# A modulation section summed in the sparse loop, a shorter burst table and an earlier branch in a one-core RG-LRU + SSD + PEER layer

## The chip, the cores and the metric

The kernel runs on one core of a Trainium2 chip. The metric is the device time of one execution in microseconds, as the median of several runs of the same program. A lower time is better. Everything is computed in float32; the large products are made from float32 weights that are split on the chip into a high and a low part.

## The reference

One layer with two sub-layers, both under adaLN modulation: a vector `c` gives six sections of 2,048 numbers each (shift, scale and gate of both sub-layers) by `silu(c) @ w_ada + b_ada`. There are 256 tokens of width 2,048.

```python
mod = silu(c) @ w_ada + b_ada                 # 6 sections of 2048
h   = rms_norm(x, norm1_g) * (1 + scale1) + shift1
proj = h @ w_in                               # RG-LRU and SSD heads
mix = concat([lru_out, ssd_out]) @ w_out      # 4096 -> 2048
x   = x + gate1 * mix
h2  = rms_norm(x, norm2_g) * (1 + scale2) + shift2
# PEER: 8 heads, product keys, 16 experts a head out of 128 * 128
act = gelu(einsum("td,thkd->thk", h2, u_tab[expert]))
out = einsum("thk,thkd->td", gate * act, v_tab[expert])
x   = x + gate2 * out                         # gate2: the last section
return rms_norm(x, final_norm_g)
```

So a token has 128 experts, and an expert is one row of `u_tab` and one of `v_tab` (2,048 floats, 8,192 bytes each). Section 5 of the kernel's `mod`, gate2, is needed only when the output of PEER is added to `x`.

## The kernel before

**Stages, in the order of the program.** First the modulation sections 0 and 1 are made on TensorE (PE). Then comes the input projection with the RG-LRU and SSD heads (to 549 us in the profile), the output projection (549 to 772 us, 64 slots: 32 that make the first 1,024 columns of the output, lines L885 to L887, and 32 for the others, L931 and L932), the queries, and PEER, which takes the rest.

**The weight pipeline.** Every 512 KB piece of a large weight is loaded by SyncE (SP) into one of four buffers `raw`, copied to a rounded high part by ScalarE (ACT, L149) and subtracted to a low part by VectorE (DVE, L158) into one of four buffers `hl`; PE then uses both parts. The subtraction of a piece frees its `raw` and so issues the load of a later piece. A stage can run ahead by what these buffers hold.

**Modulation sections 2 to 5** are sums on DVE: one step (`ada_step`, L391 and L394) loads 128 rows of 1,024 columns of `w_ada`, 512 KB, into one of two buffers `adr`, and adds them, times `c`, to the accumulator `adacc`; after 16 steps a closing of small matmuls on PE (`fin`, L403), due two slots later, sums over the 128 partitions. How often a step is taken is set by three rates: ADA_SSD and ADA_LRU steps a slot in the input projection, ADA_OUT in the output projection. The list `adq` has 7 × 16 = 112 steps: sections 2 to 4 and the first half of section 5. The second half of section 5 is summed later by `gate2_tick` (loads L1341 of 256 KB, DVE L1353 and L1355 on 128 x 512, closing L1366), in steps 32 to 63, one in each of the ticks 0 to 33 of PEER's sparse u loop but two.

**PEER in two parts.** An expert's key is its number modulo 128. Keys 0 to 99 are sparse, keys 100 to 127 dense.

- *Sparse u loop*: 25 calls of `u_quad`, each of 8 ticks, 200 ticks in all; a tick takes one 512 KB weight and makes 12 matmuls of 128 x 512 (L1496 to L1498). It makes the scores of all tokens for four keys, which are stored to DRAM: table `ad0` for keys 0 to 47, `ad1` for 48 to 99. Meanwhile DVE, ACT and PE build lists (`l_step`, `g_step`, the first around L1410 to L1425): for every block of 128 tokens (2) and group of 32 tokens (4) the entries are packed in chunks of 128, GA = 14 chunks for keys 0 to 47, and GB = 15 for keys 48 to 99. Entries that don't fit set `flag`, and a guarded branch (`spill`) adds them one token at a time.
- *Bursts*: one list chunk of all four groups is a quad, NQD = 2 × 29 = 58 of them, in the order block 0's first 14, block 1's 29, block 0's other 15. GpSimd (POOL) gathers for a quad four row buffers of 128 rows of `v_tab` (`v_feed`, L1544, up to 1 MB each, an empty slot moves nothing) and four columns of scores (`w_feed`, L1557); ACT and DVE make the burst's weights Wz from them (`w_make`: L1579, L1580, L1570, L1571), and PE does the 16 matmuls of the burst (`v_quad`, L1591; the records show 32). The function `tick` places a burst: the pacing formula with `sq["all"]`, the made weights, and two ticks after the rows were issued. Everything on POOL goes in program order, so a gather that waits for its buffer or for a stored table holds up what stands behind it. The row buffers are tk (4 of them), vq4 and vx; vq5 and vq6 are cleared (L1533) and added after the u loop.
- *Dense u*: 28 slots of two ticks each (`u_slot`, L454 and L456). *Dense v*: two halves of 28 slots (`v_slot`, L1693). Bursts go on through both; `merge` (L1720, L1722, L1725) adds a finished 128 x 512 sum to the rows in `R["t"]`; between the two halves stands the branch (L1809), after it the final RMSNorm, `final`.

The order of instructions on each engine is fixed when the program is built: what `tick`, `defer` and `mid` emit where is decided by counts, not by time. `gate2_tick`, `open_sparse` (it starts the bursts, when the lists are ready and `ad0` is stored) and `tick` are called in every tick of `u_quad`.

## Time and profile before

| what | value |
|---|---|
| runs | 2103.86, 2112.83, 2099.82 us; median 2103.86 |
| profiled execution | 2116.66 us, of which the span of the engines' work is 2114.7 |
| granted TensorE clock, mean | 0.969 |
| instructions in the span | 33,428 |
| HBM read, written | 650.45 MB, 17.34 MB |

The profiled execution is a single run, 12.8 us above the median of the others. Its own time is the span and some 2 us around it. The views that matter here are the engines' busy times; windows, which give for a stretch of time its length, each engine's busy time with the number of instructions in brackets, the granted clock of TensorE, the busy share of the DMA engines and the rate; the waits of PE by what ended them (microseconds in total, times, longest); the timeline, with the start and the length of an instruction and in square brackets the idle time before it and what ended that; and the chain of waits that ended last. PEld is the loading of weights into the array, which runs beside PE.

### The profile page before, as it was taken

The numbers are of one execution on the slowest core, as the hardware profiler recorded it, in microseconds if no ns is written. First come the engines' busy times: TensorE is split into PE (matmuls) and PEld (weight loads), VectorE is DVE, ScalarE is ACT, GpSimd is POOL, SyncE is SP. The second block draws the span as 40 slices with busy tenths as digits, with TensorE's granted clock in tenths as the row PEclk, the third lists the DMA queues.
The fourth block names the chain that finished last, engine by engine and source line by source line (L and its number), as shares of the span: only waits on it lengthen the run. The fifth ranks groups of instructions, "written<-read, shape, count | busy, mean of one in ns | idle before, by whom it ended". The sixth has DMA issues, their size and how long they took to land. (4 is left out here: it accounts for less than half of the span.)

```text
span 2114.7 us, 33428 instructions
## 1 busy us (share of the span) xinstructions
PE 1987.9 (94%) x12488; PEld 1558.1 (74%) x12488; DVE 1399.9 (66%) x2184; ACT 898.0 (42%) x1366; POOL 745.6 (35%) x629
## 2 busy tenths in 40 slices
PE   7999999999999999999999899899998799999796
PEld 4789989989998889888787466566665476666563
DVE  3378888898978778999898666565433244455444
ACT  3346666677633345444443233243232233333333
POOL 0013344322202110000011666556644566656452
PEclk9999999999999999999999899999999899999998
DMA  9967767777889965796567799999997899989993
GB/s 388 406 230 249 229 214 242 242 254 275 284 317 325 322 210 193 247 301 223 185 200 265 245 386 394 360 339 403 392 389 271 290 418 419 396 314 411 357 422 143
DMA packets 255050, 642.19 MB, mean 304 GB/s; under 512 B 28096, under 2 KB 132720, under 8 KB 227696
## 3 DMA queue, kind: packets, MB, share of 16 engines
q1 hardware_dynamic: 203408, 390.38, 53.6%
q0 software_dynamic: 40832, 215.51, 25.3%
q10 hardware_dynamic: 10640, 34.08, 4.4%
q8 instruction: 100, 1.64, 0.3%
q14 instruction: 70, 0.57, 0.1%
HBM read 650.45 MB, written 17.34 MB: 316 GB/s over the span
## 5 line engine op out<-in xcount | busy, mean ns | idle before, releaser
L149 ACT ACTIVATE hl<-raw 128x1024 fp32r<-128x1024 f32 x554 | 585.0, 1059 | 1027.2 <-PE b L1498 250.6
L158 DVE TENSOR_TENSOR hl<-raw,hl 128x1024 fp32r<-128x1024 f32 x554 | 697.8, 1263 | 354.1 <-ACT hl L149 266.9
L454 PE MATMUL b<-H,hl 128*128 128x512 f32 x1056 | 379.9, 403 | 12.4 <-DVE lsm L1570 11.4
L1496 PE MATMUL b<-hl,H 128*128 128x512 f32 x800 | 325.0, 406 | 4.5 <-ACT X L1502 4.3
L1557 POOL DMA_INDIRECT lsm<-ad,X x232 | 275.8, 1189 | 116.3 <-issue 75.3
L1498 PE MATMUL b<-hl,H 128*128 128x512 f32 x800 | 315.2, 394 | 0.0
L1497 PE MATMUL b<-hl,H 128*128 128x512 f32 x800 | 315.2, 394 | 0.0
L456 PE MATMUL b<-H,hl 128*128 128x256 f32 x1056 | 296.7, 281 | 2.4 <-DVE hl L158 2.4
L454 PEld LDWEIGHTS b<-H,hl 128*128 128x128 f32 x1056 | 199.3, 189 | 73.4 <-issue 24.5
L1591 PE MATMUL b<-tk,Wz 128*32 128x512 f32 x1072 | 226.1, 618 | 17.8 <-DMA tk<-in_v_t,X 8.1
L1544 POOL DMA_INDIRECT tk<-in_v_t,X x134 | 151.9, 1133 | 231.3 <-PE b L1591 138.7
L456 PEld LDWEIGHTS b<-H,hl 128*128 128x128 f32 x1056 | 200.3, 190 | 4.0 <-DVE hl L158 3.1
L1496 PEld LDWEIGHTS b<-hl,H 128*128 128x128 f32 x800 | 152.5, 191 | 56.5 <-issue 22.0
L1591 PE MATMUL b<-vq,Wz 128*32 128x512 f32 x520 | 186.7, 616 | 7.8 <-DMA vq<-in_v_t,X 7.8
L1498 PEld LDWEIGHTS b<-hl,H 128*128 128x128 f32 x800 | 152.3, 190 | 33.7
L1693 PE MATMUL b<-hl,X 128*128 128x512 f32 x672 | 160.9, 398 | 15.4 <-DVEq L1809 10.9
L1497 PEld LDWEIGHTS b<-hl,H 128*128 128x128 f32 x800 | 153.0, 191 | 29.4
L1693 PEld LDWEIGHTS b<-hl,X 128*128 128x128 f32 x672 | 126.5, 191 | 55.9 <-issue 24.1
L394 DVE SCALAR_TENSOR_TENSOR adacc<-adr,cact,adacc 128x1024 f32<-128x1024 f32 x105 | 142.3, 1356 | 36.2 <-DMA adr<-in_w_ada 35.8
L809 PE MATMUL b<-H,hl 128*128 128x256 f32 x560 | 161.6, 289 | 0.4 <-DVE ggt L466 0.4
L811 PE MATMUL b<-H,hl 128*128 128x256 f32 x560 | 158.4, 283 | 1.3 <-DVE hl L158 1.3
L810 PE MATMUL b<-H,hl 128*128 128x256 f32 x560 | 158.3, 283 | 0.0
(385 smaller groups left out, 3225.3 us busy)
## 6 DMA issues: line engine op xcount, KB each, us to landing
raw<-in_u_t SPq DMA_DIRECT2D x228, 512.0 KB
raw<-in_w_in SPq DMA_DIRECT2D x146, 512.0 KB
adr<-in_w_ada SPq DMA_DIRECT2D x112, 512.0 KB
adw<-in_w_ada SPq DMA_DIRECT2D x64, 512.0 KB
raw<-in_w_o SPq DMA_DIRECT2D x64, 512.0 KB
raw<-in_w_q SPq DMA_DIRECT2D x32, 512.0 KB
raw<-in_u_t ACTq DMA_DIRECT2D x28, 512.0 KB
raw<-in_v_t SPq DMA_DIRECT2D x28, 512.0 KB
```

The costliest lines, as they stand in the source:

```text
L149: act.activation(t[:, 0], r, AF.Copy)
L158: dve.tensor_sub(t[:, 1], r, t[:, 0].bitcast(FT))
L454: pe.matmul(ps, w[:, 0, c], x[:, k].rearrange("p a b -> p (a b)"), start=(k == first), stop=False, skip_group_check=True)
L456: pe.matmul(ps[:, :256], w[:, 1, c], x[:, k, 0], start=False, stop=(k == 15), skip_group_check=True)
L809: pe.matmul(ps, wh, hT[:, k, 0, :], start=(k == 0), stop=False)
L811: pe.matmul(ps, wl, hT[:, k, 0, :], start=False, stop=(k == 15))
L1496: pe.matmul(o, hh, w[:, 0, :, kk], start=(k == 0), stop=False)
L1497: pe.matmul(o, hl_, w[:, 0, :, kk], start=False, stop=False)
L1498: pe.matmul(o, hh, w[:, 1, :, kk], start=False, stop=(k == 15))
L1557: pool.indirect_dma_start(wA[:, n % 32:n % 32 + 1], None, adf[i], bass.IndirectOffsetOnAxis(ap=LW[:, tb, g, m:m + 1], axis=0), bounds_chec ...
L1591: pe.matmul(sb[c][32 * g:32 * g + 32, :], Wz[:, q % NW, g], buf[4 * q + g][:, c * 512:(c + 1) * 512], start=(m == a), stop=(m == b - 1), s ...
L1693: pe.matmul(ob[tb * 2 + c], w[:, i, s], v[:, k, c * 512:(c + 1) * 512], start=(jj == 0 and (i, k) == (0, 0)), stop=(jj == JD - 1 and k == 1))
```

## The change

Five things are edited.

1. The whole of section 5 goes to `gate2_tick`: `adq` ends with section 4 (96 steps), ADA_OUT is 0.74, and `gt` starts at step 0 in place of 32. A gate step is taken in each tick before 40 and in every second one after it, so its 64 steps last from tick 0 to tick 86. `open_sparse` waits for all 64 and for their closings to be issued.
2. GB is 14: 28 chunks in each block and 56 quads.
3. The two row buffers vq5 and vq6 are cleared and added inside the u loop, in the first tick in which the bursts are on and no list work is pending. The words "behind the gates" in the change's name mean the buffers' place in memory (`ohr`, `X01`), which the lists and gate sums used before.
4. `w_make` may begin the weights of quad `sq["n"] + 1`, one earlier; a burst has to be two ticks behind its made weights (`mt`) as well as its rows. `lsm` is 112 wide in place of 96.
5. The branch with `spill` stands between the dense u and the dense v loop, behind a `wsplit()` for slot 0. `spill` loads its own rows of x and gate2, and stores x back, before the rows for the merges are loaded.

```diff
-GA, GB = 14, 15
+GA, GB = 14, 14
...
-ADA_SSD, ADA_LRU, ADA_OUT = 0.65, 1.1, 1.0
+ADA_SSD, ADA_LRU, ADA_OUT = 0.65, 1.1, 0.74
...
-    adq = [(s, h, k) for s, h in ((2, 0), (2, 1), (3, 0), (3, 1), (4, 0), (4, 1), (5, 0)) for k in range(16)]
+    adq = [(s, h, k) for s in (2, 3, 4) for h in range(2) for k in range(16)]
...
-    lsm = pr.tile([128, 96], FT, name="lsm")
+    lsm = pr.tile([128, 112], FT, name="lsm")
...
-    gt = {"n": 32, "ld": 32, "fin": 2}
+    gt = {"n": 0, "ld": 0, "fin": 0}
...
-            gate2_tick()
-            if sq["ready"] and not sq["on"] and sq["stored"][0]:
+            if it < 40 or it % 2 == 0:
+                gate2_tick()
+            if sq["ready"] and not sq["on"] and sq["stored"][0] and gt["n"] == 64 and not pedue:
                 open_sparse()
+            if sq["on"] and not sq["rows7"] and not (bg or bg2 or any(stages)):
+                sq["rows7"] = True
+                add_row(s1.tile([128, D], FT, name="vq5", tag="ohr"))
+                add_row(keep.tile([128, D], FT, name="vq6", tag="X01"))
             tick()
...
             sq["made"] += 1
+            mt[q] = sq["it"]
...
-        if q >= NQD or q > sq["n"] or sq["w"] < 4 * q + 4 or sq["it"] < wt[q] + 6:
+        if q >= NQD or q > sq["n"] + 1 or sq["w"] < 4 * q + 4 or sq["it"] < wt[q] + 6:
...
-                and sq["g"] >= 4 * q + 4 and sq["it"] >= rt[q] + 2 and not (q == GA + GL - 1 and sq.get("rows", n) > n - 8)):
+                and sq["g"] >= 4 * q + 4 and sq["it"] >= max(rt[q], mt[q]) + 2 and not (q == GA + GL - 1 and sq.get("rows", n) > n - 8)):
...
             sp.dma_start(g2d.rearrange("o (k p) -> (o k) p", p=128), g2r)
-            add_row(s1.tile([128, D], FT, name="vq5", tag="ohr"))
-            add_row(keep.tile([128, D], FT, name="vq6", tag="X01"))
...
+    wsplit()
+    R["t"] = keep.tile([128, 4, D], FT, name="H")
+    rv = nc.values_load(flag[0:1, 0:1].bitcast(U32), min_val=0, max_val=1,
+                        skip_runtime_bounds_check_because="the comparison gives 0 or 1")
+    with tc.If(rv > 0):
+        spill()
     for h in range(2):
         for jj in range(JD):
-            if h == 1 and jj == 0:
-                rv.append(nc.values_load(flag[0:1, 0:1].bitcast(U32), min_val=0, max_val=1,
-                                         skip_runtime_bounds_check_because="the comparison gives 0 or 1"))
-                with tc.If(rv[0] > 0):
-                    spill()
-                rows_load(3)
             v_slot(h, jj)
             if h == 0 and jj in (0, 4, 12):
                 rows_load((0, 4, 12).index(jj))
+            elif h == 1 and jj == 0:
+                rows_load(3)
             tick()
```

The order of instructions moves at three places. First DVE in the output projection; `adacc` is the sum's accumulator, `hl<-raw` the weight's low part, `mod<-` an addition behind a closing, and both pieces begin at the last L719 (`ylru`). Before:

```order
L719 TENSOR_TENSOR ylru<-ggt,ylru 128x2x256 x2
L391 TENSOR_SCALAR adacc<-adr,cact 128x1024
L158 TENSOR_TENSOR hl<-raw,hl 128x1024
L394 SCALAR_TENSOR_TENSOR adacc<-adr,cact,adacc 128x1024
L158 TENSOR_TENSOR hl<-raw,hl 128x1024
L407 TENSOR_TENSOR mod<-b_6195,cc 128x8
```

After:

```order
L719 TENSOR_TENSOR ylru<-ggt,ylru 128x2x256 x2
L394 SCALAR_TENSOR_TENSOR adacc<-adr,cact,adacc 128x1024
L158 TENSOR_TENSOR hl<-raw,hl 128x1024
L394 SCALAR_TENSOR_TENSOR adacc<-adr,cact,adacc 128x1024
L158 TENSOR_TENSOR hl<-raw,hl 128x1024
L394 SCALAR_TENSOR_TENSOR adacc<-adr,cact,adacc 128x1024
L158 TENSOR_TENSOR hl<-raw,hl 128x1024 x2
```

Every fourth slot or so has two L158 in a row without a step between them, and the closing (L407 behind it) is further on.

Second DVE in the list stage of the u loop; `lists` and `two` are the packing of a list chunk, `adgx` the accumulator of a gate step. Before:

```order
L1412 TENSOR_TENSOR lists<-lists 128x232
L1414 TENSOR_TENSOR lists<-lists 128x928
L158 TENSOR_TENSOR hl<-raw,hl 128x1024 x2
L1410 TENSOR_TENSOR two<-lists 128x1024
L1412 TENSOR_TENSOR lists<-lists 128x232
```

After:

```order
L1412 TENSOR_TENSOR lists<-lists 128x224
L1414 TENSOR_TENSOR lists<-lists 128x896
L1355 SCALAR_TENSOR_TENSOR adgx<-S_8026,cact,adgx 128x512
L158 TENSOR_TENSOR hl<-raw,hl 128x1024 x2
L1410 TENSOR_TENSOR two<-lists 128x1024
```

Before, no L1355 stands in this part of the order; after, one stands in every second tick, and the two list operations are narrower by one chunk of 29.

Third POOL at the passage from the u loop to the dense u; `lsm<-ad` gathers scores, `in_v_t` rows, `vq_15039` and `vq_15041` (after: `vq_14341` and `vq_14343`) are the two buffers vq5 and vq6, and `ad_8790` (after: `ad_8731`) is the second score table. Before:

```order
L1544 DMA tk<-in_v_t,X_8083 128x2048 x2
L1557 DMA lsm<-ad_8790,X_8083 128x1 x8
L1533 MEMSET vq_15039 128x2048
L1533 MEMSET vq_15041 128x2048
L1544 DMA vq_15039<-in_v_t,X_8083 128x2048
L1544 DMA vq_15041<-in_v_t,X_8083 128x2048
L1557 DMA lsm<-ad_8790,X_8083 128x1 x2
```

After:

```order
L1549 DMA tk<-in_v_t,X_8024 128x2048 x4
L1549 DMA vq_14341<-in_v_t,X_8024 128x2048
L1549 DMA vq_14343<-in_v_t,X_8024 128x2048
L1562 DMA lsm<-ad_8731,X_8024 128x1 x6
L1549 DMA vq_10443<-in_v_t,X_8024 128x2048
L1562 DMA lsm<-ad_8731,X_8024 128x1
```

The memsets are gone from here (they stand some 38 rows earlier on POOL, in the u loop), and the rows of vq5 and vq6 come ahead of the first scores of the second table instead of behind them. The first burst is placed at tick 104 of the u loop in place of tick 102, the second at 106 in both; 25 bursts lie in the u loop in place of 26. The lines of the changed kernel are 5 to 6 higher here (a burst is L1597, a row gather L1549, a weight gather L1562).

More of the change, by code (lines that the diff above doesn't have):

```diff
@@ L1327, in q_evac @@
             bg.extend(g_step(n) for n in range(32))
-    gt = {"n": 32, "ld": 32, "fin": 2}
+    gt = {"n": 0, "ld": 0, "fin": 0}
     sq = {"n": 0, "it": 0, "w": 0, "g": 0, "gel": 0, "made": 0, "on": False, "lists": False, "stored": [False] * 2,
-          "ready": False, "all": 0}
+          "ready": False, "rows7": False, "all": 0}
     def gate2_load():
@@ L1529, in hybrid_kernel @@
     quads = ([(0, m) for m in range(GA)] + [(1, m) for m in range(GL)] + [(0, m) for m in range(GA, GL)])
-    free, buf, wt, rt = [], {}, {}, {}
+    free, buf, wt, rt, mt = [], {}, {}, {}, {}
     def add_row(x):
@@ L1705, in rows_load @@
         if n == 0:
-            R["t"] = keep.tile([128, 4, D], FT, name="H")
             sp.dma_start(R["t"][:, 3], bass.AP(tensor=g2d.tensor, offset=g2d.offset, ap=[[0, 128], [1, D]]))
@@ L1752, in hybrid_kernel @@
             bg_flush()
-            assert gt["n"] == 64 and not pedue and len(gpend) == 0 and sq["on"]
+            assert gt["n"] == 64 and not pedue and len(gpend) == 0 and sq["rows7"]
             g2p = gbank()[:16, :128]
@@ L1767, in spill @@
     def spill():
-        x = R["t"][:, 2]
+        rt_ = R["t"]
+        x, g2 = rt_[:, 2], rt_[:, 3]
         sl = pr.tile([128, 512], FT, name="sl", tag="xt")
@@ L1772, in spill @@
         ef, oa = sl[:, 67:68], sl[:, 68:69]
+        sp.dma_start(g2, bass.AP(tensor=g2d.tensor, offset=g2d.offset, ap=[[0, 128], [1, D]]))
+        for tb in range(2):
+            sp.dma_start(rt_[:, tb], x2d[128 * tb:128 * tb + 128, :])
         dve.memset(x, 0.0)
@@ L1796, in spill @@
                 s = slice(c * 512, (c + 1) * 512)
[L1797 to L1803 removed]
+                dve.tensor_tensor(b[c], b[c], g2[:, s], op=OP.mult)
+                dve.tensor_tensor(rt_[:, tb, s], rt_[:, tb, s], b[c], op=OP.add)
+            sp.dma_start(x2d[128 * tb:128 * tb + 128, :], rt_[:, tb])
+    wsplit()
[4 more added lines that the diff above has]
+        spill()
     for h in range(2):
         for jj in range(JD):
[L1806 to L1811 removed]
             v_slot(h, jj)
```

6 lines of the change are left out of this document (removed).

## The prediction

> **What bounds the kernel now.** I read the head of the page first, for the engine that is busiest.
>
> ```profile
> span 2114.7 us, 33428 instructions
> PE 1987.9 (94%) x12488; PEld 1558.1 (74%) x12488; DVE 1399.9 (66%) x2184; ACT 898.0 (42%) x1366; POOL 745.6 (35%) x629
> ```
>
> PE is the bound over all, so only two things shorten the kernel: fewer PE instructions, or fewer stalls of PE. Next the windows, cut at the stages (dense projection out of the mixer in two halves, lists, wait for the first sparse work, sparse u loop, the passage into the dense u table, dense u, the last dense v half, tail), tell where PE loses.
>
> ```profile
> core 0: us, PE busy (x) PEld busy (x) DVE busy (x) ACT busy (x) POOL busy (x), PEclk, DMA share, GB/s
> 548.90:661.20 112.30, 104.85 (x811) 103.76 (x810) 89.46 (x81) 47.65 (x56) 12.31 (x6) 0.94 0.91 321
> 661.20:772.40 111.20, 103.56 (x573) 90.20 (x571) 87.69 (x91) 44.79 (x60) 20.58 (x14) 0.94 0.87 300
> 964.60:1157.80 193.20, 188.68 (x948) 153.26 (x946) 170.77 (x272) 78.88 (x94) 20.59 (x15) 0.99 0.67 214
> 1203.00:1616.00 413.00, 389.82 (x2489) 253.84 (x2488) 210.61 (x297) 130.70 (x212) 235.60 (x196) 0.97 0.99 377
> 1616.00:1674.20 58.20, 39.08 (x215) 27.37 (x214) 14.31 (x22) 11.96 (x19) 32.89 (x30) 0.83 0.72 245
> 1674.20:1859.10 184.90, 181.85 (x1169) 127.23 (x1168) 81.86 (x136) 67.01 (x113) 121.03 (x103) 1.00 0.96 387
> 1967.10:1978.40 11.30, 0.42 (x2) 0.00 (x0) 5.88 (x9) 2.39 (x5) 2.42 (x3) 0.69 1.01 413
> 2088.00:2114.70 26.70, 9.30 (x65) 2.16 (x64) 16.28 (x33) 11.37 (x21) 1.98 (x2) 0.74 0.21 79
> ```
>
> The stretch 1616–1674 loses 19 us outright and runs at a granted 0.83; 1967–1978 is one stall. In the projection (548.9–772.4) PE looks 93% busy, but at 0.94. The waits of PE name what ended last:
>
> ```profile
> PE b L403 <- DVE adacc L394: 11.4, 4, 3.4
> PE b L454 <- DVE lsm L1570: 11.4, 1, 11.4
> PE b L1693 <- DVEq L1809: 10.9, 1, 10.9
> PE b L1591 <- DMA tk<-in_v_t,X: 8.1, 5, 3.1
> PE b L1591 <- DVE Wz L1571: 7.9, 2, 5.3
> PE b L1591 <- DMA vq<-in_v_t,X: 7.8, 1, 7.8
> PE b L1473 <- ACT Wt L1476: 7.1, 2, 6.0
> PE b L1425 <- DVE lists L1414: 7.0, 2, 3.6
> PE b L1693 <- ACT X L447: 3.1, 1, 3.1
> ```
>
> The first six are all at places that the change touches: L403 closes a modulation sum, L1809 is the branch, L1591 is a burst, and the wait of L454 stands in the passage.
>
> **Two bursts fewer.** The page gives L1591 a mean of 618 ns, which would make a burst of 32 records 19.8 us. The chain of waits shows otherwise:
>
> ```profile
> 2069.75 3.57 PE b L1591 x32
> 2093.17 0.30 DVE Wz L1571
> 2093.52 6.64 PE b L1591 x40
> ```
>
> The four 32-column groups run side by side: 32 records take 3.57 us. Two bursts: −7.1. The removed quads are the last list chunk of each token block. Counted from the reference's inputs, a 32-token group has at most 1,730 entries among keys 48 to 99, under 14·128 = 1,792; so both quads gather nothing, no entry overflows into the guarded branch, and the row traffic stays (a gathered row is 8,192 B, the lists' 26,288 entries make 215.4 MB, and the software queue moved as much):
>
> ```profile
> q0 software_dynamic: 40832, 215.51, 25.3%
> ```
>
> What they issue besides on POOL, 8 weight and 8 row gathers, leaves an engine that is 35% busy.
>
> **The projection.** Before, nearly each of its 64 slots carries one step of the modulation sum: a 512 KB load and an L394 on DVE beside the weight's own 512 KB and L158. After it is 0.74 of a step: of 61 steps 45 are left, and three closings (L403) of four. The grouped view of 548.9–772.4 and the windows show how it stands:
>
> ```profile
> L394 DVE SCALAR_TENSOR_TENSOR adacc<-adr,cact,adacc 128x1024 f32<-128x1024 f32 x58 | 78.5, 1353 | 36.2 <-DMA adr<-in_w_ada 35.8
> ...
> 564.00:580.00 16.00, 16.00 (x136) 16.00 (x135) 12.65 (x11) 12.26 (x16) 2.89 (x2) 1.00 0.92 319
> 580.00:596.00 16.00, 12.35 (x101) 11.94 (x100) 16.00 (x14) 8.35 (x9) 4.59 (x2) 0.99 0.78 260
> 596.00:612.00 16.00, 16.00 (x110) 16.00 (x111) 13.28 (x15) 3.32 (x4) 0.00 (x0) 0.79 0.94 341
> 595.18 3.08 PE L403 MATMUL b<-ones,adacc 128*128 128x1 f32 x16 [2.77 <-DVE adacc L394]
> ```
>
> Unhindered, PE does 136 matmuls in 16 us; 24 a slot make 2.82 us. A slot's 1.05 MB at 321 GB/s take 3.27 us. So the loads fall behind PE, DVE waits 36 us for them and sums late, and a closing stalls PE and leaves it at 0.79 (596–612). Removed: 16 × 0.524 = 8.4 MB, at the two halves' 321 and 300 GB/s 26 and 28 us. A slot then needs 0.91 MB, 2.84 us, PE's own pace. Value −27. Bounds: −6, when only one closing of four goes (11.4/4 of stall and 16 × 0.21 = 3.4 of clock); and −37, when the stage comes down from 223.5 us to 64 × 2.82 = 180 and three closings of 2 us each.
>
> The Trainium skill ("TensorE: Matmul & The Clock Gate", section "What's actually happening") has the array fall to half rate after an idle window of about 3.4 us. Here a stall of 2.77 us was enough for a granted 0.79, so the trace has it earlier. By the rule the three closings left, if shorter, would cost their stall alone; by the row 3.4 us more each.
>
> **The moved sums.** Those 16 steps come back as 32 gate steps of half the width, at ticks 33 to 86 of the sparse u loop, in the list stage.
>
> ```profile
> L1355 DVE SCALAR_TENSOR_TENSOR ohr<-S,cact,ohr x11: 732/745/753, 883.1 to 922.9; 128x512 f32<-128x512 f32 x11
> ```
>
> 32 × 0.745 = 23.8 us of DVE. In 964.6–1157.8 DVE is idle for 193.2 − 170.8 = 22.4 us, and PE already waits there for lists (7.0 us above). The 8.4 MB of loads fit: DMA moves 214 GB/s there. Queued behind each step on DVE are L158, on which PE's next tick rests, and the work on the lists. Bounds: 0 (four raw and four split buffers absorb 0.75 us at a time) and +24 (every step delays). The steps are spread over 54 ticks, so I take a quarter, +6. The opening of the sparse work moves from tick 102 to 104, but the second burst stays at 106; cost nothing, its cover is the weight gathers on POOL that set the second burst's end.
>
> **Row buffers.** Now two buffers are cleared and added after the u loop:
>
> ```profile
> 1634.81 3.57 POOL L1533 MEMSET vq<- 128x2048 f32 x2
> 1638.54 1.00 POOL L1544 DMA_INDIRECT vq<-in_v_t,X  x1 [0.16 <-POOL vq L1533]
> 1656.29 1.06 ACT L149 ACTIVATE hl<-raw 128x1024 fp32r<-128x1024 f32 x1 [20.57 <-remote]
> 1640.00:1645.00 5.00, 1.92 (x12) 0.94 (x16) 0.00 (x0) 0.00 (x0) 3.85 (x4) 0.52 0.16 35
> 1660.00:1665.00 5.00, 0.00 (x0) 0.00 (x0) 0.00 (x0) 0.00 (x0) 3.78 (x4) 0.57 1.05 372
> ```
>
> Eight weight gathers, the memsets, then at 1638.5 the rows for which a burst waits (7.8 us, DMA at 35 GB/s); then POOL issues the rows of both following bursts in one go, the weights' loads come behind them (ACT waits 20.6 us) and PE stalls 11.4 us more from 1657 (put down to L1570, though ACT's loads came late too), and is cold afterwards. The change adds the buffers in the u loop, at about burst 20, where nothing waits for POOL; the rows stay ahead and the flood is gone. The loss in 1616–1674 is 58.2 − 39.1 = 19.1 of stall and 39.1 × 0.17 = 6.6 of clock: 25.7. To that comes 4.3 for the last burst of the u loop, a part of the 8.1 us of waits for tk. Value −30. Bounds: −8 (the eight weight gathers, which still cannot start before the last scores are stored, stall the first burst alone as today's 7.8) and −36.
>
> **The branch.** Now it stands between the two dense v halves.
>
> ```profile
> L1809 PEldq COMPARE_BRANCH x1: 6326/6326/6326, 1965.4 to 1965.4; - x1
> ```
>
> Before, the window 1967.1–1978.4 is lost to it: 11.3 us. Ahead of the v loop its 6.3 us are paid again; but PE stalls there today for 3.1 us (L1693 waits for X, the split operand of slot 0), and that split now stands ahead of the branch: +3.2. What is late next are the four merges between the halves, hidden under the stall today:
>
> ```profile
> 2101.60 0.62 DVE b L1720
> 2102.24 0.69 DVE H L1722
> ```
>
> Four pairs are 5.2 us; PE can start on the first bank after 1.3, so 4 us come into the open. −11.3 + 3.2 + 4 = −4. Bounds: −8 (the merges overlap) and +4 (the full 10.9 again, beside today's 3.1).
>
> **Weights one burst ahead, tail.** The burst at 2093.52 waits for its Wz (5.3 and 2.6 us). After, the weights are made one burst earlier and the last burst is full, so 5 of the tail's 17 idle us go, and 2 elsewhere: −7 (−2 … −9). Other scattered stalls of the sparse u loop, where 25 bursts stand in place of 26 and buffers are eight from burst 20: −4 (+8 … −12; above nothing, as its DMA is full).
>
> **Sum.** −7.1 −27 +6 −30 −4 −7 −4 = −73: 2114.7 → 2041.6 of span, 2043.6 with the 2.0 that lie around it (2116.66). The profiled execution is 12.8 above the median of 2103.86. I take half of that as stall that the change removes anyway: 2043.6 − 12.8 + 6 = **2037**.
>
> **Rivals.**
>
> *DMA holds the sparse phase.* The phase from the first sparse work to the last dense slot moves 930.2 × 361 GB/s = 336 MB; 48 us shorter (7.1 + 30 + 4 + 7), it would need 381, more than the 377 of a stage with DMA share 0.99. Against it stands a stretch of 100 us at 420:
>
> ```profile
> 1157.80:2088.00 930.20, 864.38 (x5220) 577.35 (x5217) 443.14 (x659) 299.49 (x485) 536.91 (x458) 0.96 0.93 361
> ...
> 1700.00:1800.00 100.00, 100.00 (x643) 70.42 (x642) 44.52 (x73) 35.92 (x60) 69.50 (x55) 1.00 1.02 420
> ```
>
> If it holds, only projection, moved sums, branch and tail remain, about −32: 2103.9 − 32 = 2072. Chance 0.13. The Trainium skill ("DMA: Bandwidth & Descriptors", section "Where 436 GB/s comes from") puts HBM-to-SBUF traffic at about 358 GB/s, where this phase is now, so by it nothing in it could shrink; the 420 over 100 us disagree.
>
> *The projection doesn't speed up* (its pace is set by latency of the loads, not by bytes): −73 + 27 = −46, 2058 against the median; 0.10.
>
> *DVE becomes the bound of the lists.* 170.8 + 23.8 = 194.6 is more than the window's 193.2; for it speaks that PE waits for lists now. +24 and late gates, +30 in place of +6: 2061; 0.10.
>
> *The early buffers don't break the stall* in the passage, as the weight gathers for the second table still stand in front of the rows on POOL: −73 + 30 = −43, 2061; 0.10.
>
> *Slower: rows starve the weights' loads.* With eight buffers in the full u loop, two rows of 1.05 MB more are ahead of each raw load: 2.1 MB at 377 GB/s are 5.6 us. If each burst from the 20th to the 55th then stalls PE by half of that, 36 × 2.8 = 100 us: 2037 + 100 = 2137. It turns from 2.5 us a burst on. Against it: 1674–1859 has eight buffers, DMA at 0.96, and PE is busy 181.85 of 184.9. Chance 0.03.
>
> *It doesn't do what it says* (overflow into the branch, order unchanged): excluded by the count and the order rows; 0.01.
>
> **How the numbers follow.** My forecast has 0.53; its own range, from the bounds taken together, is 2010 to 2062. About 1% is what a measurement of this kernel can tell from no change: 2083 to 2125. All rivals but the slower one end faster alone; two together (2072 with 24 more gives 2096) fall within 1%: 0.09. Slower 0.04, faster 0.87. The range takes in the single rivals up to 2078 and down to 2006, when the large terms reach their far bounds.
>
> **What would show it.** Right: the projection ends near 745 with waits of L403 under 5 us in all; POOL clears two buffers inside the u loop; no PE wait over 5 us in the passage; one branch wait of 6 to 10 us ahead of the first dense v; q0 still 215.5 MB. Wrong: PE's waits for lists above 20 us; waits of L1597 (the burst after the change) or L454 for raw loads spread over the u loop; DMA at 0.99 with PE under 92% there; a projection still 220 us long.

## The result, and the profile after

The changed kernel takes 2047.19 us (median of 4 runs, 2039.0 to 2052.0); the kernel before, beside it, takes 2108.35 (4 runs, 2099.82 to 2116.57). The ratio is 0.9706, with a 95% interval of 0.9648 to 0.9764: 61 us less where 67 were forecast (2037 against 2103.86). The profiled execution went from 2114.7 of span to 2049.9. One of the ten runs of wider_spacing, an experiment below, took 4532.51 us, more than twice the others; its ratio leaves that run out, and its cause is not known.

The head of the page of the changed kernel:

```profile
span 2049.9 us, 33245 instructions
PE 1959.8 (96%) x12424; PEld 1543.4 (75%) x12424; DVE 1397.6 (68%) x2195; ACT 895.9 (44%) x1362; POOL 729.1 (36%) x613
q0 software_dynamic: 39424, 215.50, 25.8%
```

PE is still the busiest engine; its busy time fell by 28 us and its idle time by 37. The row traffic is 215.50 MB, as counted. The windows of the changed kernel, cut at the same events as those of before (two halves of the projection; ticks 34 to 87, 87 to 106 and 106 to 200 of the u loop; dense u; the two halves of dense v; the end):

```profile
551.80:648.20 96.40, 96.06 (x794) 95.62 (x793) 75.41 (x69) 46.64 (x55) 13.26 (x6) 1.00 0.89 312
648.20:749.70 101.50, 100.22 (x573) 87.59 (x572) 82.18 (x87) 46.43 (x62) 18.52 (x14) 0.97 0.87 305
949.30:1115.20 165.90, 158.56 (x785) 127.93 (x784) 159.55 (x259) 66.14 (x81) 11.21 (x9) 0.98 0.72 236
1115.20:1204.00 88.80, 72.55 (x383) 50.29 (x381) 58.98 (x84) 25.74 (x31) 41.02 (x33) 0.88 0.76 266
1204.00:1592.10 388.10, 371.01 (x2427) 246.95 (x2426) 204.28 (x288) 129.79 (x210) 230.41 (x190) 0.99 1.00 385
1592.10:1817.10 225.00, 216.57 (x1377) 152.16 (x1377) 96.19 (x157) 79.14 (x131) 144.25 (x122) 0.99 0.95 386
1817.10:1922.20 105.10, 104.99 (x560) 70.09 (x560) 60.24 (x93) 37.94 (x62) 58.76 (x52) 0.98 0.98 388
1922.20:2027.40 105.20, 104.34 (x563) 68.71 (x560) 46.88 (x78) 36.69 (x63) 59.27 (x52) 1.00 0.99 407
2027.40:2049.90 22.50, 8.03 (x66) 2.74 (x64) 15.71 (x30) 8.60 (x18) 1.99 (x2) 0.76 0.31 115
```

And the windows of before for the cuts that the prediction did not show:

```profile
970.80:1130.70 159.90, 155.65 (x775) 126.35 (x775) 141.35 (x229) 66.16 (x81) 11.21 (x9) 0.99 0.64 201
1130.70:1214.80 84.10, 74.15 (x378) 50.63 (x374) 56.87 (x77) 25.89 (x30) 42.09 (x33) 0.90 0.76 267
1214.80:1616.50 401.70, 381.89 (x2459) 252.57 (x2458) 205.55 (x291) 129.23 (x210) 227.76 (x190) 0.97 0.99 377
1616.50:1859.20 242.70, 220.46 (x1379) 154.31 (x1377) 96.04 (x157) 79.08 (x132) 154.02 (x133) 0.96 0.90 353
1859.20:1978.40 119.20, 105.16 (x560) 69.79 (x560) 62.77 (x97) 40.26 (x67) 63.69 (x56) 0.96 0.97 391
1978.40:2087.80 109.40, 109.36 (x591) 71.69 (x592) 44.94 (x75) 34.58 (x58) 58.72 (x54) 0.99 0.86 341
```

By stage: projection −25.6 (112.3 + 111.2 to 96.4 + 101.5), ticks 34 to 87 +6.0, ticks 87 to 106 +4.7, ticks 106 to 200 −13.6, dense u −17.7, dense v −14.1 and −4.2, end −4.4; the stages ahead of the projection and the queries make +4. That is the whole 65. The branch stands at the end of dense u in the changed kernel (7.2 us) and at the end of the first dense v half in before (10.9), so dense u without it fell by more than 17.7 and that half by less than 14.1. The waits of PE in the changed kernel:

```profile
PE b L1597 <- DMA tk<-in_v_t,X: 13.4, 3, 12.2
PE b L1496 <- ACT hl L149: 8.5, 2, 7.7
PE b L1699 <- DVEq L1812: 7.2, 1, 7.2
PE b L1425 <- DVE lists L1414: 3.5, 1, 3.5
PE b L1597 <- DVE Wz L1577: 1.7, 1, 1.7
PE b L403 <- DVE adacc L394: 1.3, 1, 1.3
```

The closings (L403) wait 1.3 us in place of 11.4. The two stalls of the passage (7.8 and 11.4) are gone. The branch is now L1812 and costs 7.2. But two waits stand here that were not forecast: 12.2 on the rows of the second burst, and 7.7 on ACT's high part in the u loop. The second one is read in the timeline around the place where the new buffers come into use (POOL, then ACT, start and length, idle time before), and in two windows of 5 us:

```profile
1488.74 3.56 POOL L1538 MEMSET vq<- 128x2048 f32 x2 [1.24 <-PE b L1473]
...
1522.00 1.06 ACT L149 ACTIVATE hl<-raw 128x1024 fp32r<-128x1024 f32 x1 [12.45 <-DMA raw<-in_u_t]
...
1515.00:1520.00 5.00, 0.40 (x2) 0.00 (x0) 0.00 (x0) 0.00 (x0) 3.57 (x4) 1.00 1.05 426
1520.00:1525.00 5.00, 1.85 (x4) 1.03 (x5) 1.23 (x1) 1.06 (x1) 1.00 (x1) 0.55 1.02 420
```

The buffers are cleared at 1488.7; from 1492 to 1518 POOL issues ten row gathers, DMA moves 426 GB/s at a share of 1.05 in 1515 to 1520, and the next weight piece lands behind them: ACT waits 12.5 us for it, PE 7.7, and the granted clock is 0.55 in the 5 us behind. That looks like the flood that the prediction saw in the passage of before, now in the u loop.

### The profile page after: what moved, and what is told of

Its sections match the earlier page's. It is cut to its first block, busy times and chain, and to the rows that moved or that the text cites. A ratio compares the mean times of both kernels' runs of the same rounds, so it can differ in the third digit from the quotient of the medians.

```text
span 2049.9 us, 33245 instructions
## 1 busy us (share of the span) xinstructions
PE 1959.8 (96%) x12424; PEld 1543.4 (75%) x12424; DVE 1397.6 (68%) x2195; ACT 895.9 (44%) x1362; POOL 729.1 (36%) x613
## 3 DMA queue, kind: packets, MB, share of 16 engines
q0 software_dynamic: 39424, 215.50, 25.8%
## 5 line engine op out<-in xcount | busy, mean ns | idle before, releaser
L158 DVE TENSOR_TENSOR hl<-raw,hl 128x1024 fp32r<-128x1024 f32 x554 | 695.6, 1260 | 331.0 <-ACT hl L149 261.8
L1562 POOL DMA_INDIRECT lsm<-ad,X x224 | 269.1, 1201 | 115.7 <-issue 78.9
L1597 PE MATMUL b<-tk,Wz 128*32 128x512 f32 x1008 | 211.1, 602 | 13.5 <-DMA tk<-in_v_t,X 13.4
L1549 POOL DMA_INDIRECT tk<-in_v_t,X x126 | 150.3, 1193 | 185.5 <-PE b L1597 74.6
L1597 PE MATMUL b<-vq,Wz 128*32 128x512 f32 x536 | 181.7, 600 | 1.8 <-DVE Wz L1577 1.7
L394 DVE SCALAR_TENSOR_TENSOR adacc<-adr,cact,adacc 128x1024 f32<-128x1024 f32 x90 | 124.2, 1380 | 22.8 <-DMA adr<-in_w_ada 22.8
```

Of the source, the lines that this page charges most:

```text
L158: dve.tensor_sub(t[:, 1], r, t[:, 0].bitcast(FT))
L1562: pool.indirect_dma_start(wA[:, n % 32:n % 32 + 1], None, adf[i], bass.IndirectOffsetOnAxis(ap=LW[:, tb, g, m:m + 1], axis=0), bounds_chec ...
L1597: pe.matmul(sb[c][32 * g:32 * g + 32, :], Wz[:, q % NW, g], buf[4 * q + g][:, c * 512:(c + 1) * 512], start=(m == a), stop=(m == b - 1), s ...
```

## The experiments

A and B below name windows as in the result: A is ticks 106 to 200 of the u loop, B the dense u. "Whole" is the median of the timed runs with the ratio to the kernel before, timed beside it. The kernel before took 2100.29, 2111.41 and 2110.52 us beside the three groups of runs; kernels of one group are compared by medians, others by ratios and by stages. The two profiles of the changed kernel, with no edit between them, differ by 0.8 us in A, by 4.6 in B and by 4.5 from tick 106 to the last dense v. B holds the branch, where it stands behind the dense u.

| kernel | whole, us | ratio (95%) | A, us | B, us |
|---|---|---|---|---|
| before | 2108.35 | 1 | 401.7 | 242.7 |
| changed | 2047.19 | 0.9706 (0.9648 to 0.9764) | 388.1 | 225.0 |
| sums_back | 2065.42 | 0.9833 (0.9803 to 0.9862) | 393.1 | 227.9 |
| buffers_late | 2047.29 | 0.9746 (0.9715 to 0.9776) | 375.0 | 236.5 |
| rows_first | 2039.70 | 0.9713 (0.9684 to 0.9742) | 392.8 | 229.8 |
| cleared_early | 2044.65 | 0.9739 (0.9705 to 0.9773) | 383.1 | 236.1 |
| changed_again | 2047.99 | 0.9692 (0.9659 to 0.9724) | 387.3 | 229.6 |
| gb14_alone | 2087.29 | 0.9894 (0.9853 to 0.9934) | 378.8 | 231.9 |
| weights_back | 2045.98 | 0.9675 (0.9642 to 0.9709) | 385.3 | 229.6 |
| rows_ahead | 2051.74 | 0.9701 (0.9666 to 0.9736) | 394.2 | 235.8 |
| wider_spacing | 2098.99 | 0.9924 (0.9895 to 0.9954) | 377.2 | 237.0 |
| two_parts | 2062.81 | 0.9767 (0.9718 to 0.9816) | 379.9 | 235.6 |
| branch_back | 2051.56 | 0.9705 (0.9657 to 0.9754) | 387.0 | 223.0 |
| two_fewer_in_u | 2052.50 | 0.9710 (0.9660 to 0.9760) | 398.8 | 228.2 |

**sums_back**: the changed kernel with the sums of before.

```diff
-ADA_SSD, ADA_LRU, ADA_OUT = 0.65, 1.1, 0.74
+ADA_SSD, ADA_LRU, ADA_OUT = 0.65, 1.1, 1.0
...
-    adq = [(s, h, k) for s in (2, 3, 4) for h in range(2) for k in range(16)]
+    adq = [(s, h, k) for s, h in ((2, 0), (2, 1), (3, 0), (3, 1), (4, 0), (4, 1), (5, 0)) for k in range(16)]
...
-    gt = {"n": 0, "ld": 0, "fin": 0}
+    gt = {"n": 32, "ld": 32, "fin": 2}
```

> The changed kernel with the modulation sums as before: ADA_OUT 1.0, the first half of section 5 in the projection, gate steps 32 to 63 alone in the sparse u loop. My account (the projection is paced by bytes, the 32 gate steps cost DVE time in the list stage): the projection (first L885 to the queries) goes from 197.8 back to about 223 us, ticks 34 to 87 from 165.9 to about 160, the whole about 17 to 20 above the changed kernel, 2065. Rival (the projection was slow for another reason, such as the moment of its closings): it stays under 206 and the whole within 8 of the changed kernel. Apart from that, ticks 87 to 106 (88.8 against 84.0 before) fall back to 84 if the gate steps delay the opening; they stay near 89 if the later first burst (tick 104, which this kernel keeps) does.

Two windows of it, the halves of the projection, and then ticks 34 to 87 and 87 to 106:

```profile
550.40:659.30 108.90, 103.29 (x811) 102.25 (x810) 87.47 (x80) 47.72 (x56) 13.09 (x6) 0.95 0.91 322
659.30:772.10 112.80, 102.29 (x571) 87.41 (x570) 90.50 (x92) 44.65 (x60) 17.89 (x14) 0.97 0.87 304
968.70:1128.30 159.60, 155.40 (x777) 126.05 (x776) 140.71 (x228) 66.15 (x81) 11.22 (x9) 0.99 0.63 202
1128.30:1215.90 87.60, 71.24 (x377) 49.49 (x373) 56.52 (x80) 25.64 (x31) 41.91 (x33) 0.88 0.76 264
```

The projection is back at 221.7 us (197.9 in the changed kernel, 192.9 when run again), with four waits of L403 (9.5 us in all), and ticks 34 to 87 are 6.3 us shorter. DMA moves 322 and 304 GB/s here as in before, 312 and 305 in the changed kernel: the rate is nearly the same and the bytes are fewer, as the sum has it. The time shows as idle PE (16.1 us here, 1.6 in the changed kernel) and as PE busy at a lower clock (205.6 and 196.3 us). The closings come back with the bytes, so this run does not tell the two apart. The whole, 2065.42, is 18 us above the changed kernel by medians and 27 to 30 by ratios. Ticks 87 to 106 stay at 87.6, so it is hardly the gate steps that lengthened them. In the kernels whose first burst stands at tick 102 they take 84.1 to 87.7 (mean of five 85.8), in the others with the second burst at tick 106 and the same order on POOL 86.6 to 89.3 (mean of six 88.3).

**buffers_late**: the two buffers cleared and added after the u loop, all else as changed.

```diff
-                add_row(s1.tile([128, D], FT, name="vq5", tag="ohr"))
-                add_row(keep.tile([128, D], FT, name="vq6", tag="X01"))
...
             sp.dma_start(g2d.rearrange("o (k p) -> (o k) p", p=128), g2r)
+            add_row(s1.tile([128, D], FT, name="vq5", tag="ohr"))
+            add_row(keep.tile([128, D], FT, name="vq6", tag="X01"))
```

> The changed kernel with the two row buffers cleared and added after the u loop, as before the change. My account (the memsets and the rows behind the second table's weight gathers make the passage stall): from the first dense u matmul to the first dense v 225.0 goes to 240 or more, with a PE wait of 7 us or more on rows and about as much behind it; the wait of 7.7 us on ACT's high part near 1515 in the u loop goes away, since no flood of rows comes there; the whole 8 to 17 above the changed kernel. Rival (the passage was healed by the wider spacing of the bursts, 25 in place of 26, or by the weights made ahead): the passage stays under 230 and the whole comes out 5 to 9 below the changed kernel, because the flood in the u loop is saved.

Its wait of PE on rows, and the timeline of POOL in the passage (start, length):

```profile
PE b L1595 <- DMA vq<-in_v_t,X: 11.2, 2, 10.9
...
1594.33 3.57 POOL L1536 MEMSET vq<- 128x2048 f32 x2
1598.06 1.41 POOL L1547 DMA_INDIRECT vq<-in_v_t,X  x1 [0.16 <-POOL vq L1536]
```

One stall of 10.9 us is in the passage, and B is 236.5, 7 to 11 more than with the buffers early (225.0 and 229.6). But A is 375.0, 12 to 13 less, and the stall near 1515 is gone. The whole is that of the changed kernel by medians, and 8 to 11 us more by ratios; by spans it is 2 below and 1 above the two profiles. My account of the passage held at its place, and the whole is not shown to gain: what the buffers save in the passage they cost in the u loop, nearly or in full. The second stall of before, the 11.4 us behind the flood, does not come back here, so something other than the buffers removed that one; it is 4.9 in wider_spacing and 2.7 in gb14_alone, where the spacing changed and the buffers did not.

**rows_first**: two quads' weights ahead until the first burst, not four.

```diff
-        while k and sq["w"] < 4 * min(NQD, sq["n"] + 4):
+        while k and sq["w"] < 4 * min(NQD, sq["n"] + (4 if sq["n"] else 2)):
```

> The changed kernel, but until the first burst only two quads' weights are gathered ahead in place of four, so that about 10 gathers of scores stand on POOL ahead of the second burst's last two row gathers and not 18. My account (at 1.3 us each these gathers hold up the rows for which the second burst waits, 12.2 us of PE wait in the changed kernel and 1.5 of half clock): that wait falls to 3 to 6 us, the whole 7 to 10 below the changed kernel. Rival (the rows take their time on the DMA engines, not on POOL, or the first burst frees the buffers too late): the wait stays over 9 us and the whole within 3.

Ticks 87 to 106 and the stretch from there to the last dense v, of this kernel and then of the changed one (run again):

```profile
1110.60:1187.40 76.80, 70.58 (x384) 50.92 (x381) 58.55 (x80) 25.63 (x30) 32.60 (x26) 0.96 0.83 293
1187.40:2020.30 832.90, 802.24 (x4922) 540.96 (x4921) 408.62 (x617) 282.55 (x465) 506.52 (x423) 0.98 0.98 385
```

```profile
1106.90:1196.10 89.20, 71.29 (x386) 49.22 (x382) 59.06 (x84) 25.68 (x31) 42.24 (x33) 0.90 0.76 265
1196.10:2024.00 827.90, 796.68 (x4921) 537.75 (x4921) 408.37 (x613) 284.63 (x464) 491.27 (x416) 0.99 0.98 386
```

The wait at the second burst was made by score gathers on POOL: with fewer of them ahead of the rows the opening is 12.4 us shorter. Five of the twelve come back behind it. The whole is 2039.7, the lowest of all medians, though its ratio is not below that of the changed kernel: the kernel before was faster beside it too. It is not shown to be a better version.

**cleared_early**: the buffers cleared in the u loop, used from its end.

```diff
-                add_row(s1.tile([128, D], FT, name="vq5", tag="ohr"))
-                add_row(keep.tile([128, D], FT, name="vq6", tag="X01"))
+                late.extend((s1.tile([128, D], FT, name="vq5", tag="ohr"), keep.tile([128, D], FT, name="vq6", tag="X01")))
+                for x in late:
+                    pool.memset(x, 0.0)
...
             sp.dma_start(g2d.rearrange("o (k p) -> (o k) p", p=128), g2r)
+            free.extend(late)
```

> The changed kernel, the two buffers cleared in the u loop as there, but only taken into use after the u loop, as before the change. It tells the memsets apart from the buffers. If the memsets on POOL (3.6 us) made the passage stall, it is as good as the changed kernel there (225 us from dense u to dense v, within 3) and the flood of rows near 1515 with its 7.7 us is gone: 5 to 9 below the changed kernel. If the order of the rows on POOL behind the second table's weight gathers did it, the passage stalls here as with the buffers added late, less 3.6 us at most: 235 to 242 us, and the whole is 3 to 12 above the changed kernel. I hold the second the likelier.

B is 236.1, as with the buffers late: the memsets are not what stalls the passage, the buffers in use are what spares it. By medians the whole is not above the changed kernel, against what I held likelier; by ratios it is 7 to 10 above. A is 383.1, and one long stall is in it (PE's wait, then ACT's timeline):

```profile
PE b L1496 <- ACT X L1502: 8.8, 2, 8.3
...
1511.82 1.06 ACT L149 ACTIVATE hl<-raw 128x1024 fp32r<-128x1024 f32 x1 [5.08 <-DMA raw<-in_u_t]
```

PE waited 8.3 us, up to 1513.4, for ACT's copy at L1502, and that stood on ACT behind the weight piece of 1511.82, which had waited for its load. So the weights' loads were late here too, though the two buffers were not in use; two_parts has a wait of 6.2 us of the same kind.

**changed_again**: no edit.

> The changed kernel once more, as the yardstick for the kernels that run with it on one chip: 0.97 of the kernel before, and a span within 10 us of 2049.9. If the stalls of 12.2 us at the second burst and of 7.7 us near 1515 were chance, they are not both there again.

Both waits are there again (12.5 and 10.5 us), so they are not chance of one execution.

**gb14_alone**: the kernel before with one number changed.

```diff
-GA, GB = 14, 15
+GA, GB = 14, 14
```

> The kernel before with GB = 14 alone: 56 quads, and with them one burst every 3.93 ticks in place of 3.79; sums, buffers, branch and weights as before. By my prediction's sum it is worth two bursts and a little spacing: the whole 7 to 11 below the kernel before, the passage from dense u to dense v stays at 240 or more with its two stalls. Rival, since the buffers added late cost the changed kernel nothing in all: the spacing, not the buffers, cured most of the sparse phase; then ticks 106 to 200 fall from 401.7 to under 390 and dense u to dense v from 242.7 to under 234, the whole 20 to 28 below.

A and B of it:

```profile
1216.50:1595.30 378.80, 369.13 (x2426) 246.72 (x2425) 208.08 (x293) 131.05 (x209) 226.47 (x186) 0.99 1.02 394
1595.30:1827.30 232.00, 219.98 (x1379) 151.73 (x1377) 96.13 (x156) 79.31 (x131) 137.29 (x122) 0.96 0.93 370
```

The rival holds. With buffers, weights and branch as before, A falls by 22.9 us and B by 10.7; the whole by 24, where my sum had 7 to 11. Its four runs go from 2075.93 to 2096.74, and the profile is of the fastest.

**weights_back**: the part on the weights undone.

```diff
-        if q >= NQD or q > sq["n"] + 1 or sq["w"] < 4 * q + 4 or sq["it"] < wt[q] + 6:
+        if q >= NQD or q > sq["n"] or sq["w"] < 4 * q + 4 or sq["it"] < wt[q] + 6:
...
-                and sq["g"] >= 4 * q + 4 and sq["it"] >= max(rt[q], mt[q]) + 2 and not (q == GA + GL - 1 and sq.get("rows", n) > n - 8)):
+                and sq["g"] >= 4 * q + 4 and sq["it"] >= rt[q] + 2 and not (q == GA + GL - 1 and sq.get("rows", n) > n - 8)):
```

> The changed kernel without the part on the weights: they are made for the next burst only, and a burst does not wait for two ticks behind them; the first burst is at tick 102 again. By my sum it costs 5 in the tail and 2 elsewhere, and it gives back up to 4 at the opening: the whole 2 to 7 above the changed kernel, tail 22.5 going to about 27. Rival, that the weights and not the spacing cured the sparse phase: ticks 106 to 200 lengthen by 8 or more over the changed kernel's 388, with PE waits on Wz inside the u loop, and the whole is 12 or more above.

Its wait of PE for made weights:

```profile
PE b L1597 <- DVE Wz L1577: 7.5, 2, 5.3
```

The end is 27.3 us and not 22.5, so the weights save 4.8 us there, where 5 were forecast; ticks 87 to 106 take 85.9 in place of 89.2. In all it is even with the changed kernel (2045.98 against 2047.99), where 2 to 7 above were expected.

**rows_ahead**: row gathers ahead of score gathers in every tick and behind every burst, with the edits of rows_first and cleared_early (the diff shows the part that is new).

```diff
-        w_feed()
-        w_make()
         v_feed()
+        w_feed()
+        w_make()
...
-            w_feed(1)
             v_feed(1)
+            w_feed(1)
```

> The changed kernel with three edits to the order on POOL: two quads' weights ahead until the first burst, row gathers ahead of score gathers in every tick, and the two buffers cleared in the u loop but used from its end. If a row gather that stands behind score gathers is the common cause of the stalls at the opening and in the passage, the opening keeps the 12 us that the edit of two quads gave there (ticks 87 to 106 under 79), the passage has no PE wait on rows over 4 us, and the whole is 15 to 22 below the changed kernel: 0.96 of before. If the transfers themselves are the limit (the row bytes are the same and DMA is full in the u loop), stalls come back within the next bursts and the whole is at most 6 below the changed kernel.

The opening kept 10 us of its gain (78.9), and all came back: A 394.2, B 235.8, the whole 2051.74. That fits the second account: what is taken away at one place stalls at the next. The first one is not tested in the passage, for there four score gathers still stand ahead of the rows on POOL (1591.4 to 1598.9), and PE waits 7.1 us for them.

**wider_spacing**: the kernel before with the pacing of 56 quads and all 58 bursts.

```diff
-        if (q < (NQD - 2) * (n - 3) // (sq["all"] - 3) and sq["made"] > q
+        if (q < (NQD - 4) * (n - 3) // (sq["all"] - 3) and sq["made"] > q
```

> The kernel before with one number changed: the pacing counts NQD - 4 in place of NQD - 2, so its bursts stand at the very ticks of the kernel with GB = 14 (25 in the u loop, gaps of four ticks where every fifth was three), while all 58 bursts and the wide lists stay; the last four bursts stand together at the end. If the spacing is what cured the sparse phase: ticks 106 to 200 fall from 401.7 to 376 to 386 and dense u to dense v from 242.7 to under 236; the end gets 7 to 15 longer (two more bursts there, each behind its weights), and the whole is 8 to 25 below the kernel before. Rival (the shorter table itself, its narrower list work or its empty gathers): ticks 106 to 200 stay above 393 and the whole is not below the kernel before.

A and B of it:

```profile
1218.80:1596.10 377.30, 369.83 (x2427) 247.31 (x2426) 204.84 (x288) 130.84 (x209) 227.56 (x186) 1.00 1.01 391
1596.10:1833.10 237.00, 221.42 (x1378) 153.51 (x1376) 96.16 (x157) 79.31 (x131) 136.54 (x122) 0.96 0.92 366
```

One number in the pacing gives A its 24.5 us, 3.6 of them for the burst that now stands behind the u loop. B falls by 5.7 to 237.0, 1 above what was expected. The end grows by 13.2 us (40.1 after 26.9), and the whole is still 0.9924 (0.9895 to 0.9954). So the u loop was cured by where the bursts stand and not by the shorter table itself.

**two_parts**: the kernel before with the sums moved and GB = 14; the edit is the union of the two diffs for these parts.

> The kernel before with two of the five parts: the modulation sums moved and GB = 14. If these two carry the gain and the buffers, the weights and the branch nearly nothing: stages as in the runs with each alone, 551.8 + 198 + 100 + 98 + 166 + 85 + 379 + 232 + 113 + 106 + 27.5 = 2056 of span, the whole 0.970 to 0.978 of before, within 10 of the changed kernel. Rival (the other three together carry what each alone does not show): 0.982 or more, as the kernel with the sums back is at 0.983 with all the others in it.

The span is 2057.3 (2056 expected), the ratio 0.9767. The two parts carry 48 of the 63 us that the changed kernel gains beside the same kernel before (2111.41 − 2047.99). The other three together make 15 by medians and 7 to 11 by spans.

**branch_back**: the branch between the two halves of dense v, in the changed kernel (the edits of `rows_load` and `spill` that go with it are left out).

```diff
-    wsplit()
-    R["t"] = keep.tile([128, 4, D], FT, name="H")
-    rv = nc.values_load(flag[0:1, 0:1].bitcast(U32), min_val=0, max_val=1,
-                        skip_runtime_bounds_check_because="the comparison gives 0 or 1")
-    with tc.If(rv > 0):
-        spill()
     for h in range(2):
         for jj in range(JD):
+            if h == 1 and jj == 0:
+                rv.append(nc.values_load(flag[0:1, 0:1].bitcast(U32), min_val=0, max_val=1,
+                                         skip_runtime_bounds_check_because="the comparison gives 0 or 1"))
+                with tc.If(rv[0] > 0):
+                    spill()
+                rows_load(3)
             v_slot(h, jj)
```

> The changed kernel with the branch between the two dense v halves, as before the change (there it also takes out the operand split ahead of it). My forecast of the move was -4 with the merges of the halves coming into the open at its new place. Both places cost one branch of 7 to 11 us of PE, by the records: dense u to dense v falls from 225 to 230 to about 217 to 222, the first dense v half rises from 105 to 113 to 119, and the whole is within 6 of the changed kernel. Rival (the merges hide the branch's cost only there): the whole is 7 or more above.

B is 223.0 and the first half of dense v 110.2: together 333.2, where the changed kernel has 330.1 and, run again, 334.1. Dense u fell and the first half rose by less than expected. The branch costs 7.1 us of PE's wait here and 7.2 and 7.3 in the changed kernel; the whole, 2051.56, is not told apart from 2047.19 and 2047.99.

**two_fewer_in_u**: pacing in two straight pieces, 23 bursts in the u loop.

```diff
-        if (q < (NQD - 2) * (n - 3) // (sq["all"] - 3) and sq["made"] > q
+        if (q < due(n) and sq["made"] > q
...
+    def due(n):
+        nu = sq["all"] - 4 * JD
+        if n <= nu:
+            return 47 * (n - 3) // (2 * (nu - 3))
+        return (47 + (2 * NQD - 51) * (n - nu) // (4 * JD)) // 2
```

> The changed kernel with its pacing slower in the u loop and faster behind it: 23 bursts in the u loop in place of 25, gaps of four and five ticks, none of three. If the bytes of the rows (about 3.85 MB a burst at 384 GB/s: 10 us) hold the u loop, ticks 106 to 200 fall from 387 by the two bursts' 7.1 us of PE and 8 to 13 of stalls, to 367 to 372, the wait of 10.5 on ACT's high part near 1515 is gone, and the stages behind, which are near full as well, get back 7 to 15: the whole is 2 to 12 below the changed kernel. If only gaps of three ticks stall (one of them is left in the changed kernel, worth 2 us): 376 to 380, and the whole is the same or up to 10 above, for bursts stand closer in the dense u and v.

The second burst stands at tick 107 here, so its wait falls into A; ticks 87 to 200 together are 465.1 us, 11.4 less than in the changed kernel run again, of which the two bursts are 7.1. Dense v gets all of it back (116.3 + 111.9 in place of 104.5 + 106.6), and the whole is 2052.5. The expectation for A alone (367 to 372) failed by that shift. With ticks 87 to 106 at the 89.2 us of the changed kernel A would be some 376, and the whole is 4.5 above: that is the second account (376 to 380, up to 10 above), by which only gaps of three ticks stall. The first, that the rows' bytes hold the u loop, failed; a wait of 6.8 us on ACT's high part is still there.

## Why the prediction came out, step by step

**The sum and its time.** Forecast −73 in the profile, measured −65; 2037, measured 2047.19. The total was good by luck: two wrong terms in it stood against each other. All signs that the prediction named for being right came true (the projection ends at 749.6, L403 waits 1.3 us, the buffers are cleared in the u loop, no wait over 5 us in the passage, one branch wait of 7.2, q0 at 215.50), and none of them could tell that the early buffers do not pay.

**Two bursts (−7.1).** The change of q0 by 0.01 MB shows that both were empty. wider_spacing and gb14_alone place their bursts alike and differ by these two and the lists' width: the end is 40.1 and 27.4 us, the wholes 2098.99 and 2087.29. So they cost some 12 us where they stand in the tail, 7.1 of PE and their waits for weights.

**The projection (−27): −25.6**, undone +24 to +29. Bytes over rate gave the right size, and the rates hardly changed; whether the fewer closings alone would do it was not tried. The closings wait 1.3 us, or not at all in the second profile of the changed kernel.

**The moved sums (+6): +6.0**, undone −6.3, in the ticks that were named. The step "cost nothing" for the opening failed, by 2 to 5 us; by the means it goes with the later first burst, from the part on the weights (85.8 us without it, 88.3 with it), and not with the sums; the ranges touch (up to 87.7, from 86.6). I had called the score gathers the cover of that shift; but they start with the opening, so that whole chain moves with it.

**The row buffers (−30): about 0** by medians and spans, up to −11 by ratios. This step failed. Its reading of the stall was right: the rows stood behind score gathers on POOL, and early buffers remove that wait. What it left out is the price in the u loop, where the DMA share is 1.00. In the four profiles with the buffers early and the branch behind dense u (the changed kernel twice, sums_back, weights_back) A is some 388 and B 228 on the mean; in buffers_late and cleared_early they are 379 and 236. So the buffers cost some 9 us in A and save some 8 in B. That the cost is the 2 MB of rows that come sooner, ahead of the weights' loads, is argued: the one stall of 7.7 us and its half clock stand where the buffers come into use, but cleared_early stalls for 8.3 us on late weights without them. I had that mechanism as the slower rival, for every burst; no profile has it at every burst.

**Other stalls of the sparse phase (−4): −27 to −30** (wider_spacing and gb14_alone, without the burst's 3.6). This is the term that was mis-sized, though by less in whole times: about −25 by wider_spacing (11.5 below the kernel before, with an end 13.2 longer) and −12 to −17 by gb14_alone (24.1 less the two bursts), for the one profile of before is 5 to 6 us above the medians beside these runs. I saw that 25 bursts would stand in the u loop and not 26, and took it as a trifle. In before, the bursts go 3.79 ticks apart, so every fifth follows its predecessor by three ticks; by the records of L1591, from the first start to the last end and counted from 0, bursts 10, 15, 20 and 25, each of them after three ticks, take 4.6, 5.9, 5.6 and 10.7 us in place of 3.6, 12 us more in all (burst 5 takes its 3.6). The longest wait in them is in burst 25 (timeline of PE):

```profile
1603.13 1.06 PE L1591 MATMUL b<-tk,Wz 128*32 128x512 f32 x1 [3.10 <-DMA tk<-in_v_t,X]
```

At 3.93 ticks one such gap is left in the u loop, before burst 17, which takes 5.1 to 6.8 us in eleven of the twelve profiles with this spacing and 4.0 in gb14_alone. wider_spacing shows that the spacing does it, with no other edit: −24.5 in ticks 106 to 200 and −5.7 in dense u. The 21 us that A loses in wider_spacing beside the burst's 3.6 are 12.3 of idle PE and 8.5 of busy time, at a clock of 1.00 in place of 0.97; 6.4 of the idle time were waits on list work (L1473, 9.8 to 3.4 us) and not on bursts. Why more went than the bursts' 12 us is not shown: one burst's rows, 3.9 MB (401.7 × 377 less 377.3 × 391 GB/s), go from a stage at 0.99 of DMA to a passage at 0.72, but two_fewer_in_u moved two more out of the u loop and gained only 4.3 us there beyond their own 7.1.

**The branch (−4): between −4 and +1,** not told from zero. The 10.9 us of before were 7.0 to 7.3 in every other kernel that has the branch at the old place, so part of that term was chance. No wait for merges came into the open: in the changed kernel the first dense v half has 104.99 of 105.10 us busy.

**Weights and tail (−7): −4.4 at the end**, as the experiment shows, and nothing measured in the whole, since the opening pays for it.

**The rival "DMA holds the sparse phase"** was half right. From tick 106 to the last dense v, before and changed:

```profile
1214.80:2087.80 873.00, 816.87 (x4985) 548.36 (x4985) 409.29 (x619) 283.15 (x466) 504.19 (x432) 0.97 0.95 368
```

```profile
1204.00:2027.40 823.40, 796.91 (x4921) 537.90 (x4921) 407.59 (x613) 283.55 (x464) 492.68 (x416) 0.99 0.98 388
```

321 and 319 MB, at 368 and 388 GB/s, so the phase could shrink. The Trainium skill ("DMA: Bandwidth & Descriptors", section "Where 436 GB/s comes from") has about 358 GB/s bind for HBM to SBUF; 388 over 823 us disagree. But from tick 87 to the last dense v the twelve profiles with this spacing, the changed kernel's two among them, take 910 to 924 us (before 957) whatever else is edited, with DMA at 0.94 to 0.96 and PE busy for 95 to 96%: rows_first, rows_ahead and two_fewer_in_u each take 10 to 12 us from one place and give 5 to 17 back at others. That DMA's rate is the bound there now fits this, but so does PE's own work: PE is busy for 868 to 877 us of that stretch, so at this clock no order of transfers could take more than 35 to 49 us from it. No run with fewer bytes was made, and two_fewer_in_u speaks against the bytes in the u loop, so the bound is not shown.

**What stays open.** Buffers, weights and branch together are worth 7 to 15 us (two_parts against the changed kernel), while none of them, undone alone, is shown to cost anything: by medians −2 to +4 us, for the buffers by ratios up to 11. buffers_late, which has the weights and the branch, is 11.6 us shorter than two_parts, which lacks them, from tick 106 to the middle of dense v, and 4.8 at the end; ahead of tick 106 it is 7.4 longer.

## What to carry to other kernels

Undo each part alone before believing which one paid: here the part that fixed the largest visible stall paid little or nothing, and the shorter table, by the change in pacing that looked like a by-product, paid 24 us. In this kernel's sparse phase, where POOL's queue holds up rows and DMA is full, a stall removed in one place was often only put off; judge such an edit by the length of the whole phase. Bytes removed over the stage's own rate was a good forecast for the projection, whose loads were late.

## What the runs showed of the hardware

A stall well under 3 us, with a closing behind it, can cost the clock. In the changed kernel the one closing that waited shows it (timeline of PE, then windows):

```profile
672.75 2.51 PE L403 MATMUL b<-ones,adacc 128*128 128x1 f32 x16 [1.28 <-DVE adacc L394]
...
664.00:680.00 16.00, 14.72 (x75) 12.85 (x74) 14.94 (x17) 6.04 (x9) 5.23 (x5) 0.81 0.86 279
```

1.28 us of wait and a closing of 16 matmuls with one column each, 2.51 us, went with half clock: 0.81 over 16 us, and 0.50 from 674 to 680. In its second profile the same closing did not wait, took 1.84 us and kept the clock at 1.00:

```profile
669.45 1.84 PE L403 MATMUL b<-ones,adacc 128*128 128x1 f32 x16
...
664.00:680.00 16.00, 16.00 (x101) 14.23 (x99) 13.39 (x15) 6.55 (x9) 2.55 (x2) 1.00 0.90 322
```

The wait does not decide it alone. In sums_back a longer one left the clock at 1.00:

```profile
706.14 1.95 PE L403 MATMUL b<-ones,adacc 128*128 128x1 f32 x16 [1.77 <-DVE adacc L394]
...
704.00:720.00 16.00, 14.22 (x89) 12.45 (x88) 11.91 (x13) 5.46 (x8) 0.74 (x1) 1.00 0.96 336
```

In the changed kernel the clock fell some 2.5 us after PE went idle (it is 0.98 from 673 to 674 and 0.50 from 674 to 675, and the wait began at 671.5). Even if the one-column matmuls count as idle, that is less than the idle window of about 3.4 us that the Trainium skill gives ("TensorE: Matmul & The Clock Gate", section "What's actually happening"), while the 3.7 us of wait and closing in sums_back (1.77 + 1.95) are more and cost nothing. What decides between the two cases stays open.
